# A two-layer decoder trunk: the plan of the MLP carried on to the end of the gate stage, and the gate's norm folded into its matrix and its sigmoid

## The chip, the cores and the metric

The kernel runs on one core of a Trainium2 chip, in one launch. The metric is device microseconds of that core, the median of several executions. TensorE (PE) multiplies and transposes, VectorE (DVE) and GpSimd (POOL) do arithmetic on tiles, ScalarE (ACT) copies, squares and evaluates functions, and SyncE (SP) issues nearly all DMA transfers. Each engine takes its instructions in the order in which the program gives them.

## What is computed

A trunk of two layers over 512 tokens of width 1024, in fp32. Each layer is a mixer (attention in layer 0, a gated short convolution in layer 1), an MLP with squared ReLU, and a gate stage. Cut to the parts that the change touches:

```python
def rmsnorm(x, g):
    return x * rsqrt(mean(x * x, axis=-1) + 1e-6) * g

def reference(x, p, norm_g, ..., w_mlp_up, w_mlp_down, w_ple_proj, w_ple_gate):
    for i in range(2):
        g = norm_g[i]
        m = mixer(rmsnorm(x, g[0]))                            # attention or convolution
        x = x + rmsnorm(m, g[1])
        f = square(relu(rmsnorm(x, g[2]) @ w_mlp_up[i])) @ w_mlp_down[i]
        x = x + rmsnorm(f, g[3])
        gate = sigmoid(rmsnorm(x, g[4]) @ w_ple_gate[i])       # 1024 x 1024
        e = (p[i] @ w_ple_proj[i]) * gate                      # 256 x 1024
        x = x + rmsnorm(e, g[5])
    return x
```

## The kernel before

**Numbers.** Every operand of a product is split in two parts of a shorter format, hi and lo, whose sum is the fp32 value. ACT makes hi (a copy that rounds), DVE or POOL makes lo (the value minus hi). `mm3` multiplies them with three matmuls: hi by hi, lo by hi, hi by lo. For a weight the parts are called `wh` and `wl`, for the transposed input of a product `hTh` and `hTl`.

**Tiles.** The tokens are four tiles `t` of 128, the width is two halves `n` of 512. The residual stream is `xd_t_n`, 128 tokens by 512. For a product by a weight its normed form has to be transposed: `turned` (L499) makes four 128x128 transposes on PE for a half, into one PSUM bank, and `keep` (L505) splits that bank into hTh (ACT, L441) and hTl (DVE, L442).

**Norms.** `squares` (L475) squares on ACT and sums over the width; `rstd` (L466) makes the reciprocal root on POOL, two small instructions (L469, L472); `scaled` (L491) multiplies the tile by the root and by the norm's weights on DVE, which gives `n_h` for the gate's norm and `n0b_h` for the next layer's first. For the sums after a block, `gained` (L545) multiplies by the weights (g3 or g5) and `residual` (L551) multiplies by the root and adds to `xd`. `pre_norm` (L509) does squares, root and scaling at once and puts the transposes off, until a number of products has been issued or someone needs them (`put_off`, `due`, `need`).

**Order.** The MLP is planned: `planned` (L1212) adds each piece of work as a `Step` (engine, cost, what it comes after, when it is due, which pages and banks it takes) to an `Agenda`, which walks a model of the engines, picks the step that is due first among the ready ones, and emits the instructions in that order; PE, DVE, ACT and POOL then run them so. The plan reaches from the first weight of the MLP to

```python
last = where["pg", l, 0, 0] + MORE          # MORE = -4
```

that is, it prepares weights until four before the first of the gate's matrix. What comes behind it, the last down group (banks `dn_7_t_n`), its sums, the norm, and all of `ple`, is written as a plain loop, and a scheduler that simulates the engines orders it. Weights are prepared there by `prepare` a number of weights ahead of their use (L441, L442).

**The gate stage** is `ple`, for blocks (t, n) in the order (0,0), (1,0), (0,1), (1,1), (2,1), (3,1), (2,0), (3,0). The first four have their projection `pp` (6 matmuls by `w_ple_proj`) made ahead, then each block takes 24 matmuls `pg` by eight weights of `w_ple_gate`, a sigmoid (L1887), the product e (L1893), squares and gain, and, once both halves of a token tile are done, root and residual. In layer 0 the next norm (n0b) and the convolution's products `c` follow; in layer 1 the last block is cut in halves (`last_block`) and the result leaves.

**Where it is in the span:** the last down group of layer 0 runs from 552.5 to 574.3 us, its gate stage to 637.5; in layer 1 from 1114.3 to 1136, and to 1198.8; the execution's span is 1205.3.

Lines: in the profile L433, L434 and L435 are the three matmuls of `mm3`, L502 the transposes, L477 the squares, L493 `scaled`, L548 `gained`, L555 `residual`, L1808 the sums of the last down group.

## Time and profile before

| | |
|---|---|
| median of 3 runs | 1208.84 us (1208.3 to 1209.94) |
| profiled execution | 1207.05 us |
| its span, from the first to the last instruction | 1205.3 us |
| granted TensorE clock, mean | 0.998 |
| PE busy | 1189.3 us (99%), 7039 matmuls |
| DVE, ACT, POOL busy | 1010.6 (84%), 839.7 (70%), 626.8 us (52%) |
| HBM traffic | 139.03 MB read, 6.37 MB written, 121 GB/s over the span |

"Busy" is the time in which at least one instruction of the engine runs; the loading of weights into the array (PEld) lies beside the matmuls. In a row of a timeline stand the start in us, the time, engine, line, operation, what it writes and from what, how many instructions the row holds, and in brackets how long the engine stood idle before it and what released it. In a row of a group stand the count, the busy time and the mean of one in ns, and the idle time before the group.

### The profile page before, as it was taken

The page shows a single profiled execution, that of the slowest core. Times are in us where ns is not written, and L with a number is a line of the kernel's source. Part 1 is how long each engine was busy: PE and PEld are TensorE (multiplying, and loading weights), DVE is VectorE, ACT ScalarE, POOL GpSimd, SP SyncE. Part 2 cuts the span into 40 slices and gives each one's busy share as a digit, 9 for nine tenths or more (in the row PEclk, how much of TensorE's full clock was granted, in tenths as well). Part 3 has the DMA queues.
Part 4 walks back from the last instruction along what each step waited for, and adds up shares of the span by engine and source line. Part 5 has one row for each costly group of instructions (what it writes and reads, how often), then busy time and mean ns, then how long its engine had stood idle before and what let it go on. Part 6 is the DMA issues. An engine that isn't in the chain of part 4 may idle for free.

```text
span 1205.3 us, 21009 instructions
## 1 busy us (share of the span) xinstructions
PE 1189.3 (99%) x7039; PEld 1054.6 (87%) x7039; DVE 1010.6 (84%) x1788; ACT 839.7 (70%) x1803; POOL 626.8 (52%) x624
## 2 busy tenths in 40 slices
PE   9999999999999999999999999999999999999997
PEld 7888887898899899988789999989889998899876
DVE  7888889587889999988777789768789999997873
ACT  6687778478787888777665533547878877877651
POOL 2035667049656855685213355226875577659310
PEclk9999999999999999999999999999999999999999
DMA  9475644624233323356223123542432434337301
GB/s 325 131 212 170 170 144 129 211 83 137 63 111 118 115 86 117 105 192 228 84 86 104 30 85 106 163 169 71 116 95 80 131 106 126 88 94 245 114 3 68
DMA packets 87324, 150.97 MB, mean 125 GB/s; under 512 B 10352, under 2 KB 18080, under 8 KB 87216
## 3 DMA queue, kind: packets, MB, share of 16 engines
q1 hardware_dynamic: 86640, 149.11, 39.6%
q8 instruction: 55, 0.90, 0.3%
q10 hardware_dynamic: 576, 0.53, 0.1%
q14 instruction: 53, 0.43, 0.1%
HBM read 139.03 MB, written 6.37 MB: 121 GB/s over the span
## 4 chain that ended last, share of the span: by engine, by line
PE 87%; ACT 3%; DVE 3%; issue 2%; POOL 2%; DMA 1%; SPq 0%; POOLq 0%; DVEq 0%; ACTq 0%
PE dn L433 9%; PE dn L434 9%; PE dn L435 9%; PE v L658 3%; PE up L435 2%; PE up L434 2%; PE up L433 2%; PE qk L435 2%; PE qk L434 2%; PE qk L433 2%; PE up_1c L435 1%; PE up_1c L434 1%; PE up_1c L433 1%; PE up_0c L435 1%; PE up_0c L434 1%
## 5 line engine op out<-in xcount | busy, mean ns | idle before, releaser
L1243 POOL TENSOR_TENSOR wl<-raw,wh 128x512 fp32r<-128x512 f32 x88 | 121.6, 1391 | 8.0 <-ACT wh L1751 8.0
L1751 ACT CAST wh<-raw 128x512 fp32r<-128x512 f32 x192 | 116.2, 622 | 0.0
L1243 DVE TENSOR_TENSOR acc<-dn,acc 128x512 f32<-128x512 f32 x168 | 108.1, 677 | 3.2 <-PE dn L435 3.0
L442 DVE TENSOR_TENSOR wl<-raw,wh 128x512 fp32r<-128x512 f32 x130 | 98.6, 797 | 9.4 <-ACT wh L441 9.1
L1751 ACT CAST wh<-dn_T 128x512 fp32r<-128x512 f32 x112 | 65.1, 585 | 35.7 <-DVE dn_T L1243 35.3
L1243 POOL TENSOR_TENSOR s<-m,d 128x256 f32<-128x256 f32 x20 | 15.1, 754 | 139.1 <-ACT m L1380 83.1
L1751 ACT CAST wh<-up_S 128x512 fp32r<-128x512 f32 x96 | 59.6, 620 | 24.5 <-POOL up_S L1243 23.9
L1243 DVE TENSOR_TENSOR wl<-dn_T,wh 128x512 fp32r<-128x512 f32 x112 | 74.7, 680 | 0.6 <-ACT wh L1751 0.5
L441 ACT CAST wh<-raw 128x512 fp32r<-128x512 f32 x130 | 73.0, 620 | 0.1
L1243 DVE TENSOR_TENSOR wl<-up_S,wb 128x512 fp32r<-128x512 f32 x96 | 63.4, 676 | 10.9 <-ACT wb L1755 10.9
L1243 DVE TENSOR_TENSOR wl<-raw,wb 128x512 fp32r<-128x512 f32 x100 | 66.2, 676 | 6.5 <-ACT wb L1755 6.5
L1243 POOL TENSOR_TENSOR up_S<-raw,raw 128x512 f32<-128x512 f32 x48 | 69.9, 1468 | 0.0
L1755 ACT CAST wb<-up_S 128x512 fp32r<-128x512 f32 x96 | 56.2, 587 | 10.6 <-DVE acc L1243 10.2
L1755 ACT CAST wb<-raw 128x512 fp32r<-128x512 f32 x100 | 58.3, 590 | 0.0
L434 PE MATMUL pg<-wh,hTl 128*128 128x512 f32 x128 | 51.0, 399 | 3.9 <-DVE hTl L442 3.9
L433 PE MATMUL up<-hTh,wh 128*128 128x256 f32 (+1 forms) x160 | 52.2, 326 | 0.0
L435 PE MATMUL up<-hTl,wh 128*128 128x256 f32 (+1 forms) x160 | 52.1, 325 | 0.0
L434 PE MATMUL up<-hTh,wl 128*128 128x256 f32 (+1 forms) x160 | 52.1, 325 | 0.0
L433 PE MATMUL pg<-wh,hTh 128*128 128x512 f32 x128 | 51.2, 400 | 0.6 <-ACT hTh L441 0.5
L435 PE MATMUL pg<-wl,hTh 128*128 128x512 f32 x128 | 50.9, 399 | 0.0
L435 PE MATMUL qk<-hTl,wh 128*128 128x512 f32 x128 | 50.6, 396 | 0.0
L433 PE MATMUL qk<-hTh,wh 128*128 128x512 f32 x128 | 50.3, 393 | 0.0
(555 smaller groups left out, 4811.6 us busy)
## 6 DMA issues: line engine op xcount, KB each, us to landing
raw<-in_wup SPq DMA_DIRECT2D x128, 256.0 KB, 2.8
raw<-in_wdn SPq DMA_DIRECT2D x128, 256.0 KB, 2.7
raw<-in_wcq SPq DMA_DIRECT2D x36, 256.0 KB, 2.8
raw<-in_wqk SPq DMA_DIRECT2D x32, 256.0 KB, 5.3
raw<-in_wpg SPq DMA_DIRECT2D x32, 256.0 KB, 3.0
g<-in_g SPq DMA_DIRECT2D x22, 256.0 KB, 5.6
prl<-neg_c SPq DMA_DIRECT2D x16, 256.0 KB, 6.2
raw<-in_wo SPq DMA_DIRECT2D x16, 256.0 KB, 4.7
```

What stands on the lines that cost most here:

```text
L433: nc.tensor.matmul(ps, a.hi, b.hi, start=start, stop=False)
L434: nc.tensor.matmul(ps, a.lo, b.hi, start=False, stop=False)
L435: nc.tensor.matmul(ps, a.hi, b.lo, start=False, stop=stop)
L441: nc.scalar.copy(hi, src)
L442: return eng.tensor_tensor(out=lo, in0=src, in1=hi.bitcast(F32), op=ALU.subtract)
L658: nc.tensor.matmul(ps[:, : V_CHUNKS[c][1]], getattr(of_x(k, t), p), getattr(ready["v", c, k], of), start=k == 0 and p == of, stop=k == KT ...
L1243: eng.tensor_tensor(out=out, in0=x, in1=y, op=op)
L1751: nc.scalar.copy(ready[key].hi[:, both], src())
L1755: nc.scalar.copy(aside[0].bitcast(F32R), src())
```

## The change

It has two parts, which come together.

**The plan.** `Agenda` now plans up to the end of the gate stage (`finish`, new in `mlp`; `MORE` = 8, counted from the last weight of the gate's matrix). The last down group, its sums, residuals, transposes, projections, gate products, sigmoids, e, squares and roots are steps with due times; in layer 1 all but the last block, which stays written out (`ple_end`). The down group's first two token tiles go by halves of its inner width: two of the four pieces for both tiles, then the other two. The transposes of tile 0 come after two projections, those of tile 1 after four, those of tiles 2 and 3 after the second and third block's products before them. The loads of g5 and g0 are steps too (`late2`); on SP's queue they stand ahead of the last five loads of the gate's matrix, where before they stood behind all sixteen and six loads of the convolution.

**The fold.** The norm's weights g4 scale the rows of `w_ple_gate`: the split of a gate weight is now a multiplication by a column of `first_g` (a tile of 128 x 24 with g0 of layer 0 and both g4), on ACT (L1915) and DVE (L1925). The reciprocal root of the gate's norm, one number a token, is applied behind the product, as the `scale` operand of the sigmoid (L1716). What is transposed is `xd` itself; the `scaled` of the gate's norm and the four loads of g4 are gone. The squares and the root (`n4q`, `n4r`) are made beside it. Lines are shifted: L513 is a transpose, L1628 hTh, L1185 every subtraction and sum of the plan (hTl, wl, acc), L559 `gained`, L1590 the residual, L488 squares.

```diff
-MORE = -4
+MORE = 8
+LATE2_AT = -8.0
+AFTER = 20
...
+    def gate_gain(l, k):
+
+        k += (l + 1) * KT
+        return first_g[:, k : k + 1]
...
-    first_g = consts.tile([P, KT], F32, tag="first_g", name="first_g")
+    first_g = consts.tile([P, 3 * KT], F32, tag="first_g", name="first_g")
...
-    def rstd(parts, name):
-
-        v, y = stat(f"{name}_v"), stat(f"{name}_y")
+    def rstd(parts, name, lasting=False):
+
+        v = stat(f"{name}_v")
+        y = small.tile([P, 1], F32, tag="lasting", name=f"{name}_y") if lasting else stat(f"{name}_y")
...
-            last = where["pg", l, 0, 0] + MORE
+            last = min(where["pg", l, 1, KT - 1] + 1 + MORE, len(order))
...
+                def added(t, tag, mg, after, sums, uses, then=lambda n: None, due=1e9):
+
+                    r, at = inverse(t, tag, sums, due), []
+                    for n in range(2):
+
+                        def add_to(n=n):
+                            nc.vector.scalar_tensor_tensor(
+                                out=xs_of(t, n), in0=mg[t, n][:, both], scalar=r[1][0],
+                                in1=xs_of(t, n), op0=ALU.mult, op1=ALU.add,
+                            )
+                            then(n)
+
+                        at.append(dve(1.05 * S, add_to, (r[0], after[n]), uses[n], shared=True, due=due))
+                    return at
...
+                def turn(t, tag, pair, also=lambda t, n, ps: None, copies=0):
+
+                    steps, hs = pair
+                    for n in range(2):
+                        src = (lambda n=n: xs[t][n]) if hs is None else (lambda n=n: hs[n])
+                        got, room = [], ("ps", f"{tag}turn{t}_{n}")
+                        step = agenda.add(
+                            "PE", 0, lambda n=n, got=got, src=src: got.append(turned(t, n, src(), tag)),
+                            (steps[n],), 0.0, clock[0], [room], pg(tag, t, n) if hs else (),
+                        )
+                        step.cost, step.keys = 4 * 0.115, ()
+                        clock[0] += step.cost
+                        to = lambda h, n=n: h[:, 4 * n : 4 * n + 4, t * P : (t + 1) * P]
+                        of = lambda got=got: got[0].rearrange("p (j c) -> p j c", j=4)
+                        hi = act(S, lambda to=to, of=of: nc.scalar.copy(to(hT.hi), of()), (step,),
+                                 [room])
+                        whole[tag, t, n] = dve(S, lambda to=to, of=of: add(
+                            to(hT.lo), of(), to(hT.hi).bitcast(F32), ALU.subtract), (hi,), [room])
...
+                    at = added(t, "mr", mg, after, sums, uses)
+                    pairs[t] = at, None
+                    sums = [psum_squares(t, i, "n4q", lambda i=i: xs_of(t, i), at[i])
+                            for i in range(2)]
+                    scales[t] = inverse(t, "n4r", sums, lasting=True)
...
+                def gate_of(t, n, early=None):
+
+                    got, room, gate = [], ("ps", f"pg{t}_{n}"), []
+                    for k in range(KT):
+                        key = ("pg", l, n, k)
+
+                        def product(k=k, key=key):
+                            if k == 0:
+                                got.append(bank(f"pg{l}_{n}_{t}"))
+                            mm3(got[0], tokens(hT, k, t), ready[key], k == 0, k == KT - 1)
+
+                        step = pe(3 * 0.227, product, [key], [whole["n4", t, k // 4]],
+                                  [room] if k == 0 else [],
+                                  pg("w", key, n=2) if n or l == 0 else ())
...
+                    def sigmoid():
+                        gate.append(page(f"gate{l}_{n}_{t}"))
+                        nc.scalar.activation(
+                            gate[0][:, both], got[0], AF.Sigmoid, scale=scales[t][1][0]
+                        )
+
+                    g_room, e_room, m_room = (pg(x, t, n) for x in ("gate", "e", "em"))
+                    sig = act(S, sigmoid, (step, scales[t][0]), [room], g_room)
...
+                for fs in (0, 1), (2, 3):
+                    for t in (0, 1):
+                        last_down(t, by_f(*fs))
+                for t in (2, 3):
+                    last_down(t, [(f, n) for n in range(2) for f in range(4)])
+                early = []
+                for i, (t, n) in enumerate(BLOCKS[:EARLY]):
+                    if i == TURNED:
+                        turn(0, "n4", pairs[0])
+                    early.append(proj_of(t, n, "sum"))
+                turn(1, "n4", pairs[1])
+                for i, (t, n) in enumerate(BLOCKS):
+                    if i in (2, 3):
+                        turn(i, "n4", pairs[i])
+                    if l == 0 and i in (5, 6):
+                        turn(i - 5, "n0b", pairs[i - 5], quarters, 1)
+                    if i < len(BLOCKS) - (l == 1):
+                        gate_of(t, n, early[i] if i < EARLY else None)
...
+                Step("DMA", 4 * 0.97, late2, (), 0.0, 1e9, pg("late2", n=2 + 2 * (l == 0)), [],
+                     False, 0),
...
+                if key == ("pg", l, 0, 0):
+                    late_steps[1].begin = LATE2_AT + use[key]
+                    agenda.steps.append(late_steps[1])
...
                 def high(key=key, src=src, n=n):
                     ready[key] = Pair(page(f"wh{n}", F32R), page(f"wl{n}", F32R))
+                    if key[0] == "pg":
+                        nc.scalar.mul(ready[key].hi[:, both], src(), gate_gain(l, key[3]))
+                        return
                     nc.scalar.copy(ready[key].hi[:, both], src())
...
                 def low(key=key, src=src, eng=nc.gpsimd if plain_up else nc.vector, aside=aside):
+                    if key[0] == "pg":
+                        nc.vector.scalar_tensor_tensor(
+                            out=ready[key].lo[:, both], in0=src(), scalar=gate_gain(l, key[3]),
+                            in1=ready[key].hi[:, both].bitcast(F32), op0=ALU.mult, op1=ALU.subtract,
+                        )
+                        return
                     of = aside[0] if aside else ready[key].hi[:, both].bitcast(F32)
                     add(ready[key].lo[:, both], src(), of, ALU.subtract, eng)
...
-            gate = page(f"gate{l}_{n}_{t}")
-            nc.scalar.activation(gate[:, :S], ps, AF.Sigmoid)
...
+        nc.scalar.activation(gate[:, :S], ps, AF.Sigmoid, scale=r)
...
-            g4.extend(gain(l, 4))
...
+        def late2():
+            g5.extend(gain(l, 5))
+            if l == 0:
+                g0.extend(gain(1, 0))
...
-    got["gT"] = got["g"][0].reshape(KT, P).T
+    got["gT"] = got["g"][[0, 4, 10]].reshape(3 * KT, P).T
```

Three places of the order, in layer 0. First DVE, from the sums and residual of token tiles 1 and 2 to tile 1's hTl. `acc_...<-dn_7_...` is a sum of the last down group, `n_p` a bank of transposes. Before:

```order
L493 SCALAR_TENSOR_TENSOR n_h_0_8188<-xd_1_0_7624,n_r_y,g_4_0_7640 128x512
L493 SCALAR_TENSOR_TENSOR n_h_1_8190<-xd_1_1_7626,n_r_y,g_4_1_7641 128x512
L548 TENSOR_TENSOR acc_4_0_4223<-acc_4_0_4223,g_3_0_7636 128x512
L548 TENSOR_TENSOR acc_5_0_4285<-acc_5_0_4285,g_3_1_7637 128x512
L555 SCALAR_TENSOR_TENSOR xd_2_0_7628<-acc_4_0_4223,mr_r_y,xd_2_0_7628 128x512
L555 SCALAR_TENSOR_TENSOR xd_2_1_7630<-acc_5_0_4285,mr_r_y,xd_2_1_7630 128x512
L493 SCALAR_TENSOR_TENSOR n_h_0_8240<-xd_2_0_7628,n_r_y,g_4_0_7640 128x512
L493 SCALAR_TENSOR_TENSOR n_h_1_8242<-xd_2_1_7630,n_r_y,g_4_1_7641 128x512
L548 TENSOR_TENSOR acc_4_1_4232<-acc_4_1_4232,g_3_0_7636 128x512
L442 TENSOR_TENSOR hTl<-n_p_0_8401,hTh 128x4x128
L548 TENSOR_TENSOR acc_5_1_4290<-acc_5_1_4290,g_3_1_7637 128x512
L442 TENSOR_TENSOR hTl<-n_p_1_8408,hTh 128x4x128
```

and now:

```order
L1590 SCALAR_TENSOR_TENSOR xd_1_1_7626<-acc_3_1_4377,mr_1_y,xd_1_1_7626 128x512
L1925 SCALAR_TENSOR_TENSOR wl_8188<-raw_8170,first_g,wh_8187 128x512
L1925 SCALAR_TENSOR_TENSOR wl_8203<-raw_8182,first_g,wh_8202 128x512
L1185 TENSOR_TENSOR hTl<-n_p_0_8248,hTh 128x4x128
L1925 SCALAR_TENSOR_TENSOR wl_8220<-raw_8196,first_g,wh_8219 128x512
L1925 SCALAR_TENSOR_TENSOR wl_8235<-raw_8205,first_g,wh_8234 128x512
L1925 SCALAR_TENSOR_TENSOR wl_8241<-raw_8224,first_g,wh_8240 128x512
L1185 TENSOR_TENSOR hTl<-n_p_1_8253,hTh 128x4x128
L1925 SCALAR_TENSOR_TENSOR wl_8260<-raw_8237,first_g,wh_8259 128x512
L1925 SCALAR_TENSOR_TENSOR wl_8281<-raw_8246,first_g,wh_8280 128x512
L1185 TENSOR_TENSOR hTl<-n_p_0_8300,hTh 128x4x128
L1185 TENSOR_TENSOR hTl<-n_p_1_8310,hTh 128x4x128
```

Both hTl of tile 1 stood behind the `n_h` of tile 2; now no `n_h` is there, and hTl of tiles 0 and 1 stand between the `wl` of the gate's matrix.

Second PE, around the transposes of tile 1. Before, they come when the first block's gate products are done, and the next block's follow:

```order
L435 MATMUL pg_0_0_8346<-wl_8106,hTh 128x512
L502 MATMUL n_p_0_8401<-ident,n_h_0_8188 128x128 x4
L502 MATMUL n_p_1_8408<-ident,n_h_1_8190 128x128 x4
L433 MATMUL pg_0_1_8441<-wh_8042,hTh 128x512
L434 MATMUL pg_0_1_8441<-wh_8042,hTl 128x512
L435 MATMUL pg_0_1_8441<-wl_8043,hTh 128x512
```

and now, with the gate's first block behind them:

```order
L445 MATMUL pp_1_1_8283<-wl_8060,wh_8036 128x512
L513 MATMUL n_p_0_8300<-ident,xd_1_0_7624 128x128 x4
L513 MATMUL n_p_1_8310<-ident,xd_1_1_7626 128x128 x4
L443 MATMUL pg_0_0_8316<-wh_8179,hTh 128x512
L444 MATMUL pg_0_0_8316<-wh_8179,hTl 128x512
L445 MATMUL pg_0_0_8316<-wl_8180,hTh 128x512
```

They moved ahead of the first block's 24 gate products.

Third ACT, around the hi part of tile 1. Before:

```order
L477 ACTIVATE junk,n_q_2_8232<-xd_2_0_7628 128x512
L477 ACTIVATE junk,n_q_2_8234<-xd_2_1_7630 128x512
L477 ACTIVATE junk,fs_3_0_8272<-acc_4_1_4232 128x512
L441 CAST hTh<-n_p_0_8401 128x4x128
L477 ACTIVATE junk,fs_3_1_8274<-acc_5_1_4290 128x512
L441 CAST hTh<-n_p_1_8408 128x4x128
```

and now:

```order
L1628 CAST hTh<-n_p_0_8248 128x4x128
L1628 CAST hTh<-n_p_1_8253 128x4x128
L1915 ACTIVATE wh_8280<-raw_8246,first_g 128x512
L1915 ACTIVATE wh_8291<-raw_8273,first_g 128x512
L1915 ACTIVATE wh_8297<-raw_8278,first_g 128x512
L488 ACTIVATE junk,n4q_1_0_8306<-xd_1_0_7624 128x512
L1628 CAST hTh<-n_p_0_8300 128x4x128
L1628 CAST hTh<-n_p_1_8310 128x4x128
```

The hi parts of the gate's matrix, the first eight of which stood ahead of the gate stage's squares before, now stand among the squares and hTh, two of the matrix's second half ahead of tile 1's hTh.

More of the change, by code (lines that the diff above doesn't have):

```diff
@@ L1214, in planned, with mlp @@
+    def mlp(l, hT, xs, g5, g0, late, late2, quarters, sent):
+        acc = {}
+        def planned(gB, waiting):
             L, R, both = slice(0, S // 2), slice(S // 2, S), slice(0, S)
@@ L1650, in last_up @@
                 return block
-            takes, lows_of = {}, {}
+            takes, lows_of, h_low = {}, {}, {}
             A = {}
@@ L1761, in planned @@
                 hi = agenda.add("ACT", S, high, mid, begin[0], uses=uses,
-                                takes=pg("w", key, n=2), spare=SPARE if use[key] < clock[0] else 4)
+                                takes=pg("w", key, n=2), spare=AFTER if n > where["pg", l, 1, KT - 1] else SPARE if use[key] < clock[0] else 4)
                 highs.append((min(use[key], use.get((*key[:3], "T4", key[-1]), 1e9)) if kind == "dn_sum" else use[key], hi, key))
```

305 lines of the change are left out of this document (150 added, 155 removed).

## The prediction

> **What bounds the kernel now.** I read the page's engine table first, then the waits of TensorE (PE), then the stretches around the two gate stages, then the instructions around the longest waits.
>
> ```profile
> PE 1189.3 (99%) x7039; PEld 1054.6 (87%) x7039; DVE 1010.6 (84%) x1788; ACT 839.7 (70%) x1803; POOL 626.8 (52%) x624
> ```
>
> PE is the bound: it is busy 99% of the span. The number of products does not change, so the change can only win PE's idle and slow time back. Of PE's waits (total, times, longest), the first row below is the longest of all, 3.9 us in two pieces, one in each layer's gate stage, for hTl, the low half of the transposed gate input; the other is in the conv stage behind the gate stage of layer 0.
>
> ```profile
> PE pg L434 <- DVE hTl L442: 3.9, 2, 2.0
> ...
> PE c L434 <- DVE wl L442: 0.4, 1, 0.4
> ```
>
> ```profile
> 552.50:574.30 21.80, 21.80 (x99) 18.04 (x98) 19.59 (x30) 14.17 (x30) 6.38 (x7) 1.00 0.70 231
> 574.30:637.50 63.20, 60.84 (x290) 49.73 (x289) 47.40 (x74) 39.49 (x95) 12.82 (x25) 1.00 0.25 79
> 1136.00:1198.80 62.80, 60.55 (x279) 49.56 (x277) 37.66 (x59) 26.22 (x63) 10.88 (x19) 0.97 0.08 28
> ```
>
> The first stretch is the last down group of layer 0; the other two are the gate stages. Columns are length, then busy time (instructions) of PE, PEld, DVE, ACT, POOL, then clock, DMA share, GB/s. In the down group PE has no gap. Each gate stage has about 2.3 us of them, and in layer 1 the granted clock is 0.97.
>
> Here is the wait of layer 0, seen from PE (with the first product of the stage and a group of transposes that waits for nothing):
>
> ```profile
> 574.29 0.39 PE L433 MATMUL pp<-wh,wh 128*128 128x512 f32 x1
> ...
> 577.01 1.03 PE L502 MATMUL n_p<-ident,n_h 128*128 128x128 f32 x8
> 577.80 0.48 PE L433 MATMUL pp<-wh,wh 128*128 128x512 f32 x1
> 578.12 0.40 PE L434 MATMUL pp<-wh,wl 128*128 128x512 f32 x1
> ...
> 586.07 1.04 PE L502 MATMUL n_p<-ident,n_h 128*128 128x128 f32 x8
> 587.34 0.51 PE L433 MATMUL pg<-wh,hTh 128*128 128x512 f32 x1 [0.24 <-ACT hTh L441]
> 589.80 0.50 PE L434 MATMUL pg<-wh,hTl 128*128 128x512 f32 x1 [1.96 <-DVE hTl L442]
> 590.14 0.39 PE L435 MATMUL pg<-wl,hTh 128*128 128x512 f32 x1
> ```
>
> Between 574.29 and 577.01 lie 12 products: 0.227 us each, PE's undisturbed pace. Eight transposes take 0.79 (577.01 to 577.80), and the first product after them is 0.09 longer (0.32). Undisturbed, eight transposes and two products would so take 0.79 + 0.32 + 0.23 = 1.34; the second group takes 586.07 to 590.14 = 4.07. The wait costs 2.73, not 1.96.
>
> And its cause, in VectorE's (DVE's) order:
>
> ```profile
> 587.13 1.42 DVE L493 SCALAR_TENSOR_TENSOR n_h<-xd,n_r_y,g 128x512 f32<-128x512 f32 x2 [1.99 <-POOL n_r_y L472]
> 589.06 0.69 DVE L442 TENSOR_TENSOR hTl<-n_p,hTh 128x512 fp32r<-128x512 f32 x1
> 586.53 0.56 POOL L472 TENSOR_TENSOR n_r_y<-n_r_v,neg_half 128x1 f32<-128x1 f32 x1
> 586.71 0.57 ACT L441 CAST hTh<-n_p 128x512 fp32r<-128x512 f32 x1
> ```
>
> hTl of token tile 1 could start when hTh is there (587.3). It starts at 589.06, because ahead of it on DVE's in-order queue stands n_h of the next tile, which sat idle 1.99 us for that tile's reciprocal root on POOL. DVE is not short of time there; it is blocked.
>
> In layer 1 the wait is the same, and something follows it:
>
> ```profile
> 1147.66 1.03 PE L502 MATMUL n_p<-ident,n_h 128*128 128x128 f32 x8
> ...
> 1151.73 0.39 PE L435 MATMUL pg<-wl,hTh 128*128 128x512 f32 x1
> 1152.24 0.63 PE L434 MATMUL pg<-wh,hTl 128*128 128x512 f32 x1
> ...
> 1155.61 0.39 PE L433 MATMUL pg<-wh,hTh 128*128 128x512 f32 x1
> 1152.20:1155.60 3.40, 3.40 (x9) 2.67 (x8) 1.66 (x3) 1.45 (x4) 0.65 (x2) 0.51 0.00 0
> ```
>
> 1147.66 to 1151.73 is again 4.07. From 1152.24 eight products then take 3.37 instead of 8 x 0.227 = 1.82, at a granted clock of 0.51: 1.55 lost. Layer 0's stage, with the same gap, kept 1.00 throughout.
>
> **The change, part by part.**
>
> *The wait.* In the new order xd itself is transposed, so nothing that waits for the gate's root stands on DVE ahead of hTl: no n_h, and the root goes into the sigmoid, some 5 us of products later. What stands there instead are the gate's weight splits (wl). The prices:
>
> ```profile
> L442 DVE TENSOR_TENSOR wl<-raw,wh 128x512 fp32r<-128x512 f32 x130 | 98.6, 797 | 9.4 <-ACT wh L441 9.1
> L450 ACT ACTIVATE wh<-raw,first_g 128x512 fp32r<-128x512 f32 x8 | 5.5, 724 | 0.2 <-DMA raw<-in_wv 0.2
> L452 DVE SCALAR_TENSOR_TENSOR wl<-raw,first_g,wh 128x512 fp32r<-128x512 f32 x8 | 5.5, 750 | 0.0
> L441 ACT CAST wh<-raw 128x512 fp32r<-128x512 f32 x130 | 73.0, 620 | 0.1
> 574.49 0.69 DVE L1808 TENSOR_TENSOR acc<-dn,acc 128x512 f32<-128x512 f32 x1 [0.83 <-PE dn L435]
> ```
>
> L450 and L452 are the operations that the gate's split becomes. Back to back, DVE's instructions overlap by some 0.08 (the two n_h at 587.13 take 1.42 together, 0.75 + 0.67), so I take 0.67 for a wl and 0.60 for a plain add or hTl (0.69 less as much). The anchor is the last sum of the down group: it waits for PE's last product at 574.49, and it stands in the new order too. Behind it come two residuals, two wl, hTl: 574.49 + 0.60 + 4 x 0.67 = 577.8. hTl's own input: transposes of tile 0 at 577.0 (12 products after the down group, as before), the first four done near 577.4, hTh at 578.0 to 578.6. I take 579.5 for its start, the late end, and 580.1 for its end. The transposes of tile 1 come 12 products later, from 580.6 to 581.5, and the first product that needs hTl stands at 581.7: 1.6 to spare. The second half follows behind three more wl (582.8) and is wanted after 12 products, at 584.4: 1.6 again. Two wl and hTl of tile 1 end at 585.3, wanted at 587.2: 1.9 to spare. The wait goes, in both layers: **-2 x 2.73 = -5.5**.
>
> What is late next? Tile 2 and 3 are transposed after 48 and 72 gate products, with residuals by my count 4 and 3 us ahead. ScalarE (ACT) has its ten squares and seven weight parts (0.75 and 0.68 each back to back, 12.3 us from 564) done by 576.5, so hTh is not held up. Nothing of PE's waits for DMA: in layer 0 the four loads of g5 and g0 are issued ahead of the last five gate weights and wait for a page that the down group frees at 574.3 at the latest; nine loads at the down group's 231 GB/s are 1.1 us each, so the last is there by some 585, and the second half of the gate's matrix is wanted from 592 on.
>
> *The clock.* No gap, no slow products after it: **-1.55** in layer 1. Its bounds are 0 and -1.55; I take the full amount, because the granted clock is 0.51 right behind the gap and 1.00 in all of the rest of the stage. The Trainium skill ("TensorE: Matmul & The Clock Gate", section "What's actually happening") says that the clock halves only after an idle window of about 3.4 us, which runs freely, so that its phase differs from run to run. By that rule a wait of 1.96 alone would not bring it down, the loss would have another cause, and the sum would be 1.55 smaller; layer 0's 1.00 speaks for the rule, the 0.51 just behind the gap against it. The same page ("Part 4: PE-mode transpose") does not count transposes as busy; with these, the hole is 1147.66 to 1151.39 with one product in it, 3.7 us, and the rule would allow the drop by chance of phase.
>
> *Smaller ones.*
>
> ```profile
> 595.87 0.40 PE L435 MATMUL pg<-wl,hTh 128*128 128x512 f32 x1
> 596.43 0.47 PE L433 MATMUL pg<-wh,hTh 128*128 128x512 f32 x1 [0.16 <-DVE hTl L442]
> ```
>
> The late hTl of tile 2 costs 595.87 to 596.43 less 0.23 = 0.33 in layer 0. The transposes, before in groups of two, four and eight, come eight at a time: three or four hitches of 0.09 fewer per layer. Together -0.6 and -0.3.
>
> ```profile
> 645.83 4.07 DVE L442 TENSOR_TENSOR wl<-raw,wh 128x512 fp32r<-128x512 f32 x3
> 649.29 0.28 PE L433 MATMUL c<-hTh,wh 128*128 128x256 f32 x1
> 649.96 0.38 PE L434 MATMUL c<-hTh,wl 128*128 128x256 f32 x1 [0.39 <-DVE wl L442]
> 1197.35 0.60 ACT L1887 ACTIVATE gate<-pg 128x512 f32<-128x512 f32 x1 [3.86 <-PE pg L435]
> 1198.14 0.42 DVE L1839 TENSOR_TENSOR e_end<-pp_end,gate 128x256 f32<-128x256 f32 x1 [2.15 <-PE pp_end L435]
> ```
>
> The conv stage behind layer 0 waits 0.67 - 0.12 = 0.55 once for a wl behind the last n0b; as its chain from the last sigmoid is shortened by about 0.6 against PE, I take **-0.4** (bounds 0 and -0.55). The sigmoid gets a per-token scale, by the weight parts' 724 against 620 some 0.10 dearer; the last one ends 0.19 ahead of e_end, which hides it: 0, or +0.1 uncovered. The fold makes 32 wh 0.10 dearer on ACT and 32 wl 0.07 on DVE, and takes 16 n_h (0.71 each, 11 us) off DVE; all beside PE, cost nothing while the spare times above hold. Four loads of g4 fewer: DMA is used 25% and 8% here, nothing.
>
> Sum: -5.5 - 1.55 - 0.9 - 0.4 = **-8.4**. The profiled execution took 1207.05 (span 1205.3 and 1.75 around it); it would become 1198.7. The three timed runs have a median of 1208.84, 1.8 above it; I predict 1208.84 - 8.4 = **1200.4**.
>
> **Rivals.**
>
> *The clock term stays* (the rule above, or a slow stretch that comes from elsewhere), perhaps the conv wait too: -5.5 - 0.9 = -6.4 gives 1202.4; with the conv wait gone 1202.0.
>
> *hTl is late again, now behind wl.* The price of a wl on DVE is not constant: three of them took 4.07 in the conv stage (1.36 each), beside large additions on POOL. In the gate stage POOL has 25 instructions of 0.5 us, which speaks against it. If a wl cost 0.9 to 1.0, the five ahead of the second half would use up the 1.6, and a wait of about 1 us would stay in each layer, with the clock term: 1200.4 + 2 + 1.55 = 1204.
>
> *VectorE becomes the bound, slower than before.* At 1.36 for each wl of the gate stage, its 16 per layer add 16 x 0.69 = 11.0; 1.7 of it is spare, 9.3 lands on PE. Two layers: 1200.4 + 18.6 = 1219. The change breaks even where 16 x extra - 1.7 = 4.2, an extra of 0.37, that is 1.04 for a wl. The row of 130 (mean 797, with POOL's disturbance in it) stays below that.
>
> *The wait moves, no gain.* ACT runs hTh of tile 1 behind two weight parts of the matrix's second half. If their loads came later than 584 instead of some 15 us earlier, PE would stand at the same place for the same reason as before, 1208.8. In the down group DMA is used 70%, not full.
>
> **How the numbers follow.** What this kernel's runs can tell from no change is about 0.2%, 2.4 us. My forecast (1200.4, own range 1199 to 1202) gets 0.66, the clock or conv term that stays 0.16, the wl wait 0.08, no gain 0.06, slower 0.04. All of the first two and most of the third lie below 1206.4: faster 0.88, same 0.08, slower 0.04. The range reaches up to 1205.2, past the wl wait; what lies above it is no gain and slower, 0.10. Below, the conv wait's other bound gives 1200.2, and since the three runs before lie 1.25 to 2.9 above the profiled execution, a median 1.8 closer to it gives 1198.4; I leave about 0.08 below that.
>
> **What would show it.** Right: no PE wait for hTl in either gate stage; hTl of tile 1 done before its transposes' first product; clock 1.00 in layer 1's gate stage; that stage 4.5 shorter, layer 0's about 3.5; wl rows near 750, and a conv wait under 0.3. Wrong: wl of the gate stage over 900, a PE wait for hTl or wl in the stage's first 15 us, a clock under 0.98 there, or a wait for a load of the gate's matrix.

## The result, and the profile after

The changed kernel takes 1199.63 us (median of 6 runs, 1199.41 to 1199.94) against 1208.51 for the kernel before (6 runs, 1205.74 to 1209.94): a ratio of 0.9931, 95% interval 0.992 to 0.9941. Two more sets of five runs gave 1201.05 (0.9948, 0.9934 to 0.9961) and 1199.90 (0.9933, 0.9921 to 0.9946). Predicted were 1200.4. The profiled execution took 1199.94, with a span of 1198.2.

First the page's engine line and the waits of PE (total, times, longest):

```profile
PE 1186.0 (99%) x7039; PEld 1054.0 (88%) x7039; DVE 1002.7 (84%) x1772; ACT 841.9 (70%) x1803; POOL 629.1 (53%) x624
```

```profile
PE warm_p L2056 <- DVE warm L2038: 1.5, 1, 1.5
PE ps_o L806 <- ACT ph L787: 1.2, 1, 1.2
PE v L669 <- ACT wh L460: 0.9, 1, 0.9
PE c L444 <- DVE wl L452: 0.7, 1, 0.7
```

No wait for hTl is left; the longest wait behind the attention is now that of the conv stage, 0.7 where it was 0.4. Next the two gate stages (same columns as before: PE, PEld, DVE, ACT, POOL, clock, DMA share, GB/s):

```profile
574.30:634.20 59.90, 59.90 (x290) 50.11 (x289) 44.72 (x70) 40.21 (x91) 11.05 (x20) 1.00 0.30 94
1133.00:1191.90 58.90, 58.23 (x279) 48.62 (x277) 36.57 (x58) 27.92 (x61) 10.19 (x16) 1.00 0.11 36
```

PE has no gap in the first, and in the second only the 0.7 us by which the window reaches past its last product; the clock is 1.00 in both. Layer 0's stage took 3.3 us less (63.2 to 59.9); layer 1's, from its first projection (1135.88, now 1133.00) to its last product (1198.47, now 1190.96), took 4.6 less. On VectorE the same work as in the prediction's sum:

```profile
574.62 0.69 DVE L1185 TENSOR_TENSOR acc<-dn,acc 128x512 f32<-128x512 f32 x1 [0.35 <-PE dn L445]
575.23 1.41 DVE L1590 SCALAR_TENSOR_TENSOR xd<-acc,mr_y,xd 128x512 f32<-128x512 f32 x2
576.55 1.41 DVE L1925 SCALAR_TENSOR_TENSOR wl<-raw,first_g,wh 128x512 fp32r<-128x512 f32 x2
578.59 0.69 DVE L1185 TENSOR_TENSOR hTl<-n_p,hTh 128x512 fp32r<-128x512 f32 x1 [0.63 <-ACT hTh L1628]
579.20 2.07 DVE L1925 SCALAR_TENSOR_TENSOR wl<-raw,first_g,wh 128x512 fp32r<-128x512 f32 x3
581.18 0.68 DVE L1185 TENSOR_TENSOR hTl<-n_p,hTh 128x512 fp32r<-128x512 f32 x1
581.78 1.40 DVE L1925 SCALAR_TENSOR_TENSOR wl<-raw,first_g,wh 128x512 fp32r<-128x512 f32 x2
583.11 1.28 DVE L1185 TENSOR_TENSOR hTl<-n_p,hTh 128x512 fp32r<-128x512 f32 x2
```

hTl of tile 0 ends at 579.3 and 581.9, that of tile 1 at 584.4; the prediction had 580.1, 582.8 and 585.3. The split with a factor costs what the attention's rows said (columns: shortest, median, longest in ns), the sigmoid with its scale 0.09 more than the 598 of before:

```profile
L1925 DVE SCALAR_TENSOR_TENSOR wl<-raw,first_g,wh x32: 736/743/751, 573.5 to 1151.3; 128x512 fp32r<-128x512 f32 x32
L1915 ACT ACTIVATE wh<-raw,first_g x32: 706/714/740, 571.9 to 1144.6; 128x512 fp32r<-128x512 f32 x32
L1716 ACT ACTIVATE gate<-pg,n4r_y x15: 668/688/690, 588.6 to 1183.0; 128x512 f32<-128x512 f32 x15
```

What went the other way is the conv stage behind layer 0. First come rows of the changed kernel's timeline (VectorE, POOL and PE), then rows of the kernel before (POOL, VectorE):

```profile
636.48 1.42 DVE L504 SCALAR_TENSOR_TENSOR n0b_h<-xd,n0br_y,g 128x512 f32<-128x512 f32 x2 [0.45 <-POOL n0br_y L483]
638.35 1.42 DVE L1590 SCALAR_TENSOR_TENSOR xd<-em,er_y,xd 128x512 f32<-128x512 f32 x2 [0.45 <-POOL er_y L483]
...
643.09 4.06 DVE L452 TENSOR_TENSOR wl<-raw,wh 128x512 fp32r<-128x512 f32 x3
...
636.54 0.86 POOL L480 TENSOR_SCALAR er_v<-es,es 128x1 f32<-128x1 f32 x1
637.48 0.84 POOL L483 TENSOR_TENSOR er_y<-er_v,neg_half 128x1 f32<-128x1 f32 x1
...
647.21 0.39 PE L444 MATMUL c<-hTh,wl 128*128 128x256 f32 x1 [0.71 <-DVE wl L452]
```

```profile
640.11 0.30 POOL L469 TENSOR_SCALAR er_r_v<-es,es 128x1 f32<-128x1 f32 x1 [2.97 <-ACT junk L477]
640.49 0.56 POOL L472 TENSOR_TENSOR er_r_y<-er_r_v,neg_half 128x1 f32<-128x1 f32 x1
...
641.09 1.42 DVE L555 SCALAR_TENSOR_TENSOR xd<-em,er_r_y,xd 128x512 f32<-128x512 f32 x2 [1.17 <-POOL er_r_y L472]
```

Tile 3's root (`er`) on POOL runs beside n0b_h of tile 2 and takes 0.86 + 0.84, where it took 0.30 + 0.56 with VectorE at rest. Tile 3's residual starts 4.1 us after the first conv product (634.21), where it was 3.6 (637.48). PE loses 1.26 us in the conv stage instead of 0.74. Here and below, what PE loses "by its starts" is the time from one start to the next beyond the undisturbed pace, added up over a stage.

### The profile page after: what moved, and what is told of

Its sections match the earlier page's. It is cut to its first block, busy times and chain, and to the rows that moved or that the text cites. A ratio compares the mean times of both kernels' runs of the same rounds, so it can differ in the third digit from the quotient of the medians.

```text
span 1198.2 us, 20984 instructions
## 1 busy us (share of the span) xinstructions
PE 1186.0 (99%) x7039; PEld 1054.0 (88%) x7039; DVE 1002.7 (84%) x1772; ACT 841.9 (70%) x1803; POOL 629.1 (53%) x624
## 4 chain that ended last, share of the span: by engine, by line
PE 94%; ACT 2%; issue 1%; DVE 1%; DMA 1%; POOL 0%; SPq 0%; POOLq 0%; DVEq 0%; ACTq 0%
PE dn L444 9%; PE dn L443 9%; PE dn L445 9%; PE v L669 3%; PE up L445 2%; PE up L444 2%; PE up L443 2%; PE pg L445 2%; PE pg L443 2%; PE pg L444 2%; PE qk L445 2%; PE qk L444 2%; PE qk L443 2%; PE up_1c L445 1%; PE up_1c L444 1%; PE up_1c L443 1%
## 5 line engine op out<-in xcount | busy, mean ns | idle before, releaser
L1185 DVE TENSOR_TENSOR acc<-dn,acc 128x512 f32<-128x512 f32 x184 | 119.0, 678 | 10.5 <-PE dn L445 10.1
L1185 POOL TENSOR_TENSOR wl<-raw,wh 128x512 fp32r<-128x512 f32 x88 | 121.4, 1387 | 8.0 <-ACT wh L1917 8.0
L1917 ACT CAST wh<-raw 128x512 fp32r<-128x512 f32 x208 | 124.5, 622 | 0.0
L1185 POOL TENSOR_TENSOR s<-m,d 128x256 f32<-128x256 f32 x20 | 15.1, 753 | 139.2 <-ACT m L1322 83.1
L452 DVE TENSOR_TENSOR wl<-raw,wh 128x512 fp32r<-128x512 f32 x82 | 68.0, 862 | 8.8 <-ACT wh L451 8.5
L1185 DVE TENSOR_TENSOR wl<-dn_T,wh 128x512 fp32r<-128x512 f32 x112 | 74.7, 680 | 0.6 <-ACT wh L1917 0.5
L1185 DVE TENSOR_TENSOR wl<-up_S,wb 128x512 fp32r<-128x512 f32 x96 | 63.3, 676 | 11.1 <-ACT wb L1921 11.1
L1185 POOL TENSOR_TENSOR up_S<-raw,raw 128x512 f32<-128x512 f32 x48 | 69.8, 1466 | 0.0
L1185 DVE TENSOR_TENSOR wl<-raw,wb 128x512 fp32r<-128x512 f32 x100 | 66.2, 676 | 4.1 <-ACT wb L1921 4.1
L444 PE MATMUL qk<-hTh,wl 128*128 128x512 f32 x128 | 50.2, 392 | 0.0
```

The source lines that it names most:

```text
L444: nc.tensor.matmul(ps, a.lo, b.hi, start=False, stop=False)
L452: return eng.tensor_tensor(out=lo, in0=src, in1=hi.bitcast(F32), op=ALU.subtract)
L1185: eng.tensor_tensor(out=out, in0=x, in1=y, op=op)
L1917: nc.scalar.copy(ready[key].hi[:, both], src())
```

## The experiments

**1. The plan alone.** Theory A said that the order removes the wait, theory B that the fold does.

```diff
-                    pairs[t] = at, None
-                    sums = [psum_squares(t, i, "n4q", ...) ...]
-                    scales[t] = inverse(t, "n4r", sums, lasting=True)
+                    pairs[t] = normalised(t, "n4", lambda: g4, at)    # n_h as before, planned
...
-                            gate[0][:, both], got[0], AF.Sigmoid, scale=scales[t][1][0]
+                            gate[0][:, both], got[0], AF.Sigmoid
```

> The plan to the end of the gate stage, without the fold: n_h is scaled by root and g4 on VectorE as before, the gate's weights are split without a factor, the sigmoid has no scale. Theory A (the order is what removes the wait): the two waits for hTl of 2.73 us each are gone all the same, since tile 1's n_h is now planned ahead of its transposes and hTl of tile 0 and 1 stand ahead of tile 2's n_h; some 0.7 us stays in layer 0 before tile 2's transposes, whose squares stand behind the first sigmoid and its table load. Time 1200 to 1201.5. Theory B (the fold is what removes it, by taking the root out of the chain and 11 us off VectorE): the squares, root and n_h, some 4 us, stay in front of each tile's transposes, PE waits 1 to 2.7 us in each layer, and the slow clock behind the wait stays: 1203 to 1207.

Measured: 1206.55 (11 runs, 1205.73 to 1207.75) against 1207.42 of the kernel before beside it, ratio 0.9993 (0.9984 to 1.0002). The plan alone gains nothing that can be told from no change. Here are the waits of PE in the first 30 us of the two gate stages, layer 0 first, and then rows of VectorE in layer 0, where n_h of the next tile stands for POOL's root:

```profile
PE pg L445 <- DVE wl L1185: 0.8, 2, 0.6
PE n_p L513 <- DVE n_h L504: 0.4, 2, 0.3
```

```profile
PE n_p L513 <- DVE n_h L504: 1.4, 2, 1.1
PE pg L445 <- DVE wl L1185: 0.5, 2, 0.2
```

```profile
588.76 1.88 DVE L1185 TENSOR_TENSOR wl<-raw,wh 128x512 fp32r<-128x512 f32 x3
591.49 1.42 DVE L504 SCALAR_TENSOR_TENSOR n_h<-xd,n4r_y,g 128x512 f32<-128x512 f32 x2 [0.85 <-POOL n4r_y L483]
```

The long wait for hTl is gone, as theory A had it, but the transposes now wait for n_h and the products for wl: by PE's starts 3.9 us are lost in layer 0's stage and 4.1 in layer 1's. The kernel before lost 4.0 and 5.1 in its profiled execution, 1.55 of the 5.1 by the slow clock. Theory A falls.

**2. The fold alone**, in the order of the kernel before; run in two sets.

```diff
+            elif key[0] == "pg":
+                split_gained(hi, lo, raw, w, (key[1] + 1) * KT + key[3], eng, False)
...
+            scales[t] = rstd(sums, f"{name}_r{t}", True)
+            hs = xs
...
+            nc.scalar.activation(gate[:, :S], ps, AF.Sigmoid, scale=scales[t])
```

> The fold alone in the kernel before: xd is transposed, g4 goes into the gate's rows, the root into the sigmoid; the order from the last down group on is the scheduler's as before. Theory A: the block by n_h is gone, but another in-order block comes in its place: hTl of tile 1's second half stands behind e of the first block, which waits for the first sigmoid and, in layer 0, its table load; by the order PE then waits 1 to 1.5 us in layer 0 and about 0.5 in layer 1. Time 1202 to 1204.5. Theory B (the fold does it all): no wait left, 1200.

> The fold alone in the old order once more, beside the changed kernel. If the plan has a share of its own, it stays 1 to 2.5 us above the changed kernel, with PE's lost time in the two gate stages near 1 and 2.7 us against 0.5 and 0.4; if the fold does it all, the two agree within 0.5.

Measured: 1202.22 (ratio 0.9958, 0.9945 to 0.9972) and 1202.73 (0.9957, 0.9945 to 0.997); the changed kernel beside the second set took 1199.90. The fold gives about two thirds of the gain by itself. The plan gives the rest, 2.8 us, and only together with the fold. The block that was expected in layer 0 is there, here in VectorE's timeline of the second run; below it stand the longest waits of PE in layer 1:

```profile
588.35 0.69 DVE L1902 TENSOR_TENSOR e<-pp,gate 128x512 f32<-128x512 f32 x1 [1.83 <-ACT gate L1896]
588.96 1.41 DVE L564 SCALAR_TENSOR_TENSOR xd<-acc,mr_r_y,xd 128x512 f32<-128x512 f32 x2
590.28 0.68 DVE L445 TENSOR_TENSOR hTl<-n_p,hTh 128x512 fp32r<-128x512 f32 x1
```

```profile
PE n_p L506 <- DVE e L1902: 0.6, 1, 0.6
PE pg L436 <- ACT hTh L444: 0.4, 1, 0.4
```

VectorE stands 1.83 us for the first sigmoid, with a residual and hTl behind it. That costs less than expected: layer 0's stage is only 0.6 us longer than in the changed kernel, and PE waits there for the residual, not for hTl. In layer 1, where I first expected the smaller loss, the stage is 2.3 us longer. PE's waits there are for e and hTh, and this loss was not foreseen.

**3. VectorE's load put back.** What does the fold save: VectorE's time, or the root and scaling between residual and transposes?

```diff
+                        def extra(j=j):
+                            h = page(f"extra{l}_{t}_{j}")
+                            nc.vector.scalar_tensor_tensor(
+                                out=h[:, both], in0=xs_of(t, j), scalar=neg_half, in1=xs_of(t, j),
+                                op0=ALU.mult, op1=ALU.mult,
+                            )
```

> The changed kernel with VectorE's load of the kernel before put back and nothing else: for each token tile two multiplications of 128x512 of xd by itself, into a page that nothing reads, due at the tile's transposes, in place of the n_h that the fold removed (8 per layer, 5.4 us). No root stands ahead of them and PE waits for none of them. Theory A (the fold pays because VectorE is full in the first 30 us of the gate stage: busy 27.4 of 30 us in the changed kernel): PE loses 1.5 to 3 us in each layer, waits for wl of the matrix's second half as with the plan alone; 1202.6 to 1205.5. Theory B (it pays because the root and the scaling stand between residual and transposes): no loss, 1199.4 to 1200.4.

> The load on VectorE again (eight multiplications of 128x512 per layer that nothing reads, due where n_h was due with the plan alone), now with the right pages in the down group's last sums: in the first form one half of each tile's sum went to the page of another product. Theory B (the root and scaling in the chain cost, not VectorE's time): as in the first form, about 1 us of wait for a wl near 598 us in layer 0 and 0.2 in layer 1, time within 1.5 us of the changed kernel beside it. Theory A (VectorE is full): 3 us or more slower than the changed kernel beside it.

Measured: the first form 1201.08 with the changed kernel at 1201.05 beside it, the second 1201.52 against 1199.90. (In the first form one half of each token tile's last sum went to another product's page, which makes its results wrong; the second form has the right pages.) In both, PE waits once for a wl, near 598 us in layer 0 (first form, then second):

```profile
PE pg L445 <- DVE wl L1938: 0.6, 1, 0.6
PE pg L445 <- DVE wl L1938: 0.4, 1, 0.4
```

It loses 0.9 us (first form: 1.0) more than in the changed kernel there, and 0.2 more in layer 1. So by PE's starts 1.1 to 1.2 us hang on VectorE's time, by the medians 0.0 and 1.6, which is short of theory A's 3. The plan alone loses 6.9 us more than the changed kernel in the two gate stages. What the load does not explain, more than 5 us, is left by difference for the chain of squares, root and scaling, as theory B said; no run puts that chain back alone. The two are not wholly apart either. A root is two POOL instructions, and they are slower beside a busy VectorE: in the plan alone tile 2's first one took 1.40 us (from 589.41) ahead of n_h, and in the second load run it took 3.47 (from 590.23), where PE waited for nothing behind it, as only the sigmoid needs the root.

**4. The hole filled.** Does the spread of the kernel before come from the clock behind its hole, the stretch in which PE stands?

```diff
+            if (t, n) == (1, 0):
+                for _ in range(10):
+                    nc.tensor.matmul(
+                        ps, tokens(hT, 0, 0).hi, ready["pg", l, 0, 0].hi, start=True, stop=True
+                    )
```

> The kernel before, with ten extra matmuls that nothing uses (128x512, 2.27 us in all) put on PE behind tile 1's transposes in both gate stages, where PE waited 2.2 us for hTl; they write a bank that the next real product overwrites. The wait for hTl is the same, PE is only not idle in it. Theory A (the hole makes the clock drop, in one layer or both, differently from run to run, and this is why the kernel before spreads over 4 us): no slow products behind it, a granted clock of 1.00 in both stages, runs within 1 us of each other, median near the lowest of before, 1205.5. Theory B (the slow products have another cause): clock drop and spread as before, median 1208.5 or up to 0.5 more.

Measured: 1209.33 (11 runs, 1207.91 to 1211.45), ratio 1.002 (1.0011 to 1.0029), which neither theory had. The clock did stay at 1.00 behind the filled holes, but the scheduler gave another order in the conv stage, where PE now loses 3.6 us instead of 0.7 (the clock is the third number from the right):

```profile
588.00:594.00 6.00, 5.83 (x29) 4.46 (x28) 4.34 (x8) 2.04 (x5) 2.23 (x4) 1.00 0.00 1
648.00:655.00 7.00, 5.16 (x41) 4.75 (x40) 7.00 (x9) 7.00 (x19) 6.11 (x4) 1.00 0.39 99
1152.00:1158.00 6.00, 5.83 (x28) 4.42 (x28) 4.35 (x8) 2.54 (x7) 2.37 (x4) 1.00 0.00 0
```

As a test of the spread it failed: it closed two holes and opened others. The eleven runs still spread over 3.5 us (the kernel before beside them 3.8), and their mean granted clock is 0.998 as before. So no run shows that the spread comes from the gate stages' holes.

**5. Holes put in**, in the changed kernel: the tile of a block is transposed once more to the same place and its hTl written several times, ahead of four blocks of each gate stage.

```diff
+                            hi = whole[tag, t, n] = dve(...)         # 2 times in layer 0, 4 in layer 1
...
+                    if i in (1, 4, 5, 6):
+                        turn(t, "n4", pairs4[t], times=2 + 2 * l)
```

> The changed kernel with eight holes made on purpose: ahead of four blocks of each gate stage the tile is transposed once more to the same place, and its hTl is written twice (layer 0) or four times (layer 1), with the same values. PE stands behind the transposes for about 1.5 us in layer 0 and 2.5 to 3 us in layer 1, that is 2.5 and 4 us from the transposes' start with one product in it (it was 3.7 in the kernel before). Theory A (such a hole can bring the clock down, by the phase of whatever watches it): one to three of the four in layer 1 are followed by some 8 products at half pace, none or one in layer 0. Theory B (the slow products behind the wait of layer 1 in the kernel before had another cause): none in either. Time about 1199.6 + 4 x 2.5 + 4 x 4 = 1225, and 1.5 more for each drop.

Measured: 1258.17 in the one run, where 1225 and 1.5 for each drop was expected. All eight holes were longer than meant (2.5 us from the transposes' start in layer 0, 4 in layer 1), since hTh and hTl came late. The table gives the time from the transposes' start to the third product, where 1.34 is undisturbed; the groups of 622.78 and 638.26 hold sixteen transposes, and 0.79 of their time is taken off as well:

| transposes from | to the third product, us | of it lost, us | slow products behind |
|---|---|---|---|
| six groups of transposes without a wait | 1.33 to 1.34 | 0 | none |
| 599.59 and 1186.73 | 1.6 | 0.2 to 0.3 | none |
| 612.57 | 3.80 | 2.5 | none |
| 587.58, 1214.98, 1228.80 | 5.4 to 5.8 | 4.0 to 4.5 | 7, 7, 8 |
| 622.78, 638.26 | 6.7, 7.3 | 4.6, 5.2 | 12, 6 |
| 1172.69, 1199.68 | 6.9, 6.4 | 5.6, 5.1 | 11, 12 |

The stretches behind three of them (the long one of 587.58, the one of 612.57, the long one of 622.78):

```profile
593.60:597.00 3.40, 3.40 (x9) 2.64 (x9) 3.40 (x6) 1.33 (x3) 0.00 (x0) 0.50 0.57 119
616.00:619.50 3.50, 3.47 (x15) 2.86 (x16) 3.50 (x6) 0.25 (x1) 0.08 (x1) 1.00 0.00 0
629.40:634.50 5.10, 5.10 (x13) 3.96 (x12) 0.02 (x1) 0.00 (x0) 0.00 (x0) 0.50 0.00 0
```

All seven holes that lost 4 us or more were followed by 6 to 12 products at 0.427 instead of 0.227 us, 1.2 to 2.4 us in all; the one that lost 2.5 was not. So a hole brings the clock down, as theory A had it, though in this run it did so every time at these lengths, where theory A had only some of them. The holes of the kernel before lost 2.73 each, and one of the two was followed by slow products. No hole of that length came out here, so how often it happens there stays open.

**6. The conv stage: n0b_h of tile 2 later.**

```diff
-                        steps.append(dve(1.05 * S, scale, (r[0],), ...
+                        steps.append(dve(1.05 * S, scale, (r[0], *behind), ...   # tile 2: tile 3's residual
```

> The changed kernel with one step moved: the scaling n0b_h of token tile 2 in layer 0 comes on VectorE behind the last residual of tile 3 instead of ahead of it. Theory A (the conv stage's wait of 0.88 us came from the two small POOL instructions of tile 3's root, which took 0.86 and 0.84 beside VectorE's scaling where they take 0.30 and 0.56 alone): they are 0.3 and 0.56 again, tile 3's residual and n0b_h come about 0.9 to 1.1 us earlier against PE, and PE's wait in the conv stage falls from 0.88 to under 0.2: 0.7 to 0.9 us faster than the changed kernel, 1198.8. Theory B (the wait hangs on the wl themselves, 1.36 us each beside POOL's sums): the wait stays near 0.8 and so does the time, 1199.6.

Measured: 1201.82 (1200.31 to 1202.11), no gain; by PE's starts the conv stage loses 1.0 us more than in the changed kernel. The root of tile 2 (`n0br`) stays ahead of tile 3's on POOL, and its first instruction now takes 1.26 beside e and wl, so tile 3's residual starts 4.0 us after the first conv product, where it was 4.1. With one more wl in the row PE waits twice:

```profile
636.23 1.26 POOL L480 TENSOR_SCALAR n0br_v<-n0bq,n0bq 128x1 f32<-128x1 f32 x1 [5.03 <-DVE e L1727]
638.22 0.30 POOL L480 TENSOR_SCALAR er_v<-es,es 128x1 f32<-128x1 f32 x1
638.61 0.56 POOL L483 TENSOR_TENSOR er_y<-er_v,neg_half 128x1 f32<-128x1 f32 x1
644.12 5.77 DVE L452 TENSOR_TENSOR wl<-raw,wh 128x512 fp32r<-128x512 f32 x4
```

```profile
PE c L444 <- DVE wl L452: 1.4, 2, 0.7
```

It is seen again that POOL's pair takes 0.30 and 0.56 with VectorE at rest. It is not shown that PE waited because of it: the pair is short here, and PE waits longer.

**7. More of the convolution in the plan, and tile 3's root first.**

```diff
-MORE = 8
+MORE = 12
```

> The changed kernel with its plan carried on over twelve weights of the convolution instead of eight, so that four more splits are planned ahead of tile 3's norm. Theory A (PE's wait of 0.9 us in the conv stage is for the three wl that stand behind tile 3's n0b_h on VectorE and take 1.36 us each beside POOL's sums): the wl are made earlier, alone, at 0.6 each, and the wait falls to under 0.3: 0.6 to 0.9 us faster than the changed kernel in the same call, near 1198.9. Theory B (the wait is set by tile 3's chain of residual, squares, root and n0b_h, and the wl only stand last): those four push the chain back or the next weights wait instead, and the time is the changed kernel's within 0.3.

> The changed kernel once more, unchanged, beside the others on one chip. Expected: 1199.4 to 1200.5 in every run, no wait for hTl, one wait of 0.7 to 0.9 us for a wl in the conv stage, and a spread under 1.5 us where the kernel before has some 4. If its spread is as wide as that of the kernel before, the narrow first six runs were chance.

Measured: 1199.97 (1199.71 to 1201.88) against 1201.05 (1200.17 to 1202.91) of the changed kernel beside it; the two ranges overlap. The expectation for the changed kernel itself failed here: its runs spread over 2.7 us where under 1.5 was expected, so the 0.5 us of its first six runs is not its usual spread (the third set has 1.1). By PE's starts the conv stage loses 1.01 instead of 1.26; the wait moved from the wl to the transposes, which wait for n0b_h:

```profile
PE n0b_p L513 <- DVE n0b_h L504: 0.4, 1, 0.4
```

Then the second edit, on top of the first (tile 2's last root after tile 3's root and residual):

```diff
+                    r[0].after += behind      # tile 2: tile 3's root and residual
```

> The changed kernel with its plan over twelve weights of the convolution, and with tile 2's last root (n0b) behind tile 3's root and residual on POOL and VectorE. Theory A (POOL's small instructions, 0.86 beside VectorE's multiplications against 0.3 and 0.56 alone, hold tile 3's chain up): tile 3's residual starts within 3.2 us of the first conv product instead of 4.1, its n0b_h 0.4 to 1 us earlier, and what PE loses in the conv stage falls from 1.26 (changed kernel) and 1.0 (twelve weights alone) to under 0.6; 0.5 to 0.9 us faster than the changed kernel beside it. Theory B: the slow instructions only move to tile 2's or tile 3's n0b root, which now run beside the residual and n0b_h; the loss stays near 1.0 and the time within 0.4 of the changed kernel.

> The changed kernel, unchanged, as the measure for the three beside it. 1199.4 to 1203; what it spreads comes from two places in the MLP, near 425 to 475 and 975 to 1025 us, where its profile one time lost 1.4 us and the other time nothing, in stages that the change does not touch.

Measured: 1199.43 (1198.63 to 1200.69) against 1199.90 (1199.43 to 1200.56), ratio to the kernel before 0.9929 (0.9917 to 0.9942) against 0.9933. PE loses 0.27 in the conv stage, but not for theory A's reason: the POOL pair is as slow as ever and the residual later still, 4.4 us after the first conv product (633.73).

```profile
636.38 0.81 POOL L480 TENSOR_SCALAR er_v<-es,es 128x1 f32<-128x1 f32 x1 [6.68 <-ACT junk L488]
637.27 0.85 POOL L483 TENSOR_TENSOR er_y<-er_v,neg_half 128x1 f32<-128x1 f32 x1
638.15 1.42 DVE L1591 SCALAR_TENSOR_TENSOR xd<-em,er_y,xd 128x512 f32<-128x512 f32 x2 [0.45 <-POOL er_y L483]
...
643.93 3.42 DVE L452 TENSOR_TENSOR wl<-raw,wh 128x512 fp32r<-128x512 f32 x2
```

What PE no longer waits for is wl: two of them stand behind n0b_h instead of three, as the weights of its next products were split ahead. This version has the lowest median of those run, but the half microsecond is not separated from the changed kernel's runs.

## Why the prediction was right, and where not

- **The wait, -5.5: right, with its cause.** No wait for hTl in either stage; the spare times came out at 2.6 to 2.9 us instead of 1.6 to 1.9 (hTl of tile 0 done at 579.28, its first product at 581.87; tile 1's at 584.39 for 587.32), as hTl could start 0.9 earlier than at the late end I took. What I did not weigh is that the order needs the fold: with n_h in the chain the plan alone (experiment 1) loses in new waits what it saves.
- **The clock, -1.55: right in size on average, its place argued.** In the profiled execution one hole of two was followed by the slow clock, so the term could have been nothing or twice as much; other runs of the kernel before show a mean clock from 0.995 to 0.999. Over 39 runs of the kernel before the mean granted clock was 0.9973, over 16 of the changed one 0.9986; 0.0013 x 1205 = 1.6 us, though that mean does not tell which stage it comes from. The plan alone, which loses about as much in the gate stages but in waits of at most 1.1 us, has 0.9985 against 0.9976 beside it, which speaks for the long holes; experiment 4, with the holes filled, has 0.998, which does not, but it had others. The Trainium skill's rule of about 3.4 us of idle time ("TensorE: Matmul & The Clock Gate", "What's actually happening") agrees with experiment 5, where holes that lost 4 us or more were always followed by the slow clock and the one of 2.5 was not; the 2.73 of the kernel before lies below it and still had it once, which the rule allows only if the transposes ahead are not counted as work.
- **Hitches, -0.9: right.** By PE's starts they gave 0.7 and 0.4. Behind each group of eight transposes the first product is 0.09 longer, four times in each stage and twice more for n0b in layer 0; the other hitches and the 0.33 of tile 2 are gone.
- **The conv stage, -0.4: wrong in sign.** It lost 0.5 more. The step that failed is "its chain from the last sigmoid is shortened by about 0.6 against PE": e of tile 3 does come 0.6 earlier against PE, but tile 3's root first stands behind tile 2's on POOL, 0.3 of the 0.6, and then runs beside n0b_h of tile 2, 0.86 + 0.84 instead of 0.30 + 0.56. So the residual comes 0.5 later, and so does all that follows it. I had priced POOL's pair from rows in which VectorE was at rest. Of what takes the wait away, only splitting the next wl earlier was shown (experiment 7); a faster pair was not shown to: in experiment 6 tile 3's pair took 0.30 + 0.56 again and the residual was hardly earlier.
- **The sigmoid's scale and the fold's dearer splits, 0: right in the stages.** At the end, from the start of e_end to the end of the span, kernels with the fold took 7.4 to 7.6 us and those without 7.2. In all of them the last store is issued 4.4 us after e_end and lands at 6.3, so the difference lies behind that. Its cause is not settled.
- **Sum.** By the two profiled executions: -3.3 and -4.6 in the gate stages, +0.5 in the conv stage, +0.4 at the end, 7.0 of the 7.1 by which the span shrank, where 8.4 was forecast: the conv stage and the end make the difference. The medians gave -8.9, -7.2 and -8.4 in the three sets. That they lie around the forecast is in part luck: the profiled execution of the kernel before was 1.5 us under its median, that of the changed kernel 0.3 above its own.
- **The rivals.** A wl of the gate stage cost 0.74, so neither the wait for hTl behind wl nor VectorE as the bound came true; PE waited for no load of the gate's matrix.

## What to carry to other kernels

A step that waits for a chain must not stand in an in-order queue ahead of one that does not: the price is the whole rest of the chain, plus what PE's clock does behind the hole. Taking a factor per row into the weights and a factor per token behind the product removes that chain from PE's path, and only then was there something for a better order to win. The two halves of the fold, and the parts of the new order, were not run apart. When a small instruction is on the path, price it from rows in which its neighbours are as busy as they will be.

## What the runs showed of the hardware

POOL's pair of one-column instructions took 0.30 and 0.56 us with VectorE at rest. Where VectorE worked beside it, the same two took 0.8 to 0.9 each in the conv stage of the changed kernel and up to 1.57 and 1.67 in the gate stages of the plan alone. In the second load run one took 3.47, from 590.23 to 593.70, that is until 0.17 behind the end (593.53) of a row of VectorE's multiplications without a gap.

A hole on PE is paid twice from some length on: in the one run of experiment 5, holes that lost 4 us or more cost another 1.2 to 2.4 us each at a granted clock of 0.50.

And the MLP, which the change does not touch, has a place in layer 0 that loses 1.3 us more in some executions than in others:

```profile
PE dn L444 <- DVE A22l L1185: 0.4, 1, 0.4
```

This is the changed kernel's second profile, between 425 and 475 us; the first profile has no such wait there. It may be a part of why the kernel's runs reach from 1199.4 to 1202.9; its cause was not looked for.
